# Rotary products from GpSimd to VectorE, and conv taps dealt out anew between the score groups, in a two-layer decoder trunk

## The chip, the cores and the metric

The kernel runs on one core of a Trainium2 chip. The metric is the device time of one execution in microseconds (us). The engines of the core work side by side, each through its own list of instructions in a fixed order: TensorE (PE, with its weight loads PEld), VectorE (DVE), ScalarE (ACT), GpSimd (POOL) and SyncE (SP, which issues DMAs).

## The reference

Two layers over 512 tokens of width 1024, batch 1, in fp32. `q`, `k`, `v`, `u_conv` and `q_mem` are columns of one projection.

```python
for l in range(2):
    h = x + 0.5 * swiglu(rms_norm(x, ffn1_norm[l]), ffn1_w1[l], ffn1_w3[l], ffn1_w2[l])
    n = rms_norm(h, mix_norm[l])
    u_conv, q, k, v, q_mem = split(n @ w_in[l])
    y_conv = silu(layer_norm(causal_depthwise_conv31(glu(u_conv)) + b, g, b2))     # 384 channels
    q = apply_rope(rms_norm(q per head), cos, sin)                                 # 6 heads of 64
    k = apply_rope(rms_norm(k per head), cos, sin)                                 # 2 heads of 64
    y_swa = sliding_window_attention(q, k, v, sinks)                               # blocks of 128
    y_mem = memory_attention(rms_norm(q_mem per head), mk, mv)                     # 4 heads, 256 memory tokens
    h = h + concat(y_conv, y_swa, y_mem) @ w_out[l]
    h = h + 0.5 * swiglu(rms_norm(h, ffn2_norm[l]), ffn2_w1[l], ffn2_w3[l], ffn2_w2[l])
    x = rms_norm(h, final_norm[l])

def apply_rope(x, cos, sin):
    x1, x2 = split(x, 2, axis=-1)
    return concatenate([x1 * cos - x2 * sin, x2 * cos + x1 * sin], axis=-1)
```

## The kernel before

The activations stay on the chip, channels across the 128 partitions and the 512 tokens along them; the weights stream in. Each fp32 product is three passes of TensorE (`mm3`, L176 to L178): an operand is split into a rounded high part and the rest, and hi·hi, hi·lo and lo·hi are summed. A weight tile is split in one of two ways. `split` (L145, L146) rounds on ScalarE and subtracts on VectorE. `split_by_dma` (L150 to L152) rounds on ScalarE, writes the negative on ScalarE as well, and lets a DMA that POOL issues add the raw weights onto it. Activations are split by `split_scaled` (L155 on ScalarE, L156 on VectorE).

A layer is FFN1, the mixer, FFN2. The mixer takes from about 364 to 545 us in layer 0 and 1247 to 1430 us in layer 1. `ORDER` is the list of its steps, and every engine's instructions are issued by a scheduler that follows this list, its queues and the edges that `tc.issue_after` adds:

- `c` projects half a chunk of conv channels; `q` projects a block of 128 tokens' queries and keys and applies the rotary (L701 evacuates, L706 is the product with the sine table on POOL with the halves of each head exchanged, L710 the one with the cosine table, L712 their sum); `Q` transposes them;
- `v` projects a block's values and memory queries (L733, L735 and L548 on ScalarE evacuate them); `V` transposes the memory queries (L581, evacuated by L583);
- `g` begins a group of scores. There are ten groups, of the memory ("r") and of the window ("w"). A group is a few score matmuls (L769, after the mask's L763), maxima on VectorE (L773, L788), and one or two small operations (L774, or L789 and L790) that make the bias of its exponentials (L800);
- `a` is the attention over the groups: exponentials, transposes of the probabilities (L810, evacuated by L812), products with the values (L821), and where a block is complete the division (L830 to L835), its transposes (L844) and the split of the result. `out_weights(d)` fetches and splits the rows of the output weights for the attention's channels, `out_rows` multiplies them;
- `t` adds one chunk's 31 taps of the conv on VectorE (L932 and 30 of L939, over 512 tokens). `EARLY` taps run freely; of the others each is held behind the bias of one group, as many as `LATER` says for it;
- `s` sums the three chunks on POOL (L945 and the line before), takes their mean on TensorE (L950), variance, scale (RL, L221), and Silu.

A step written early can be worked in while TensorE does another, so the order on the engines is not simply that of `ORDER`. The projected weights of the queries, `wqk`, are split by `split_by_dma` for three of their four tiles (hi and lo are called ghi and glo). `Next` prepares the mixer's input while FFN1 ends: for each d the residual h (L475), its split and its Square (L236) for the norm. `factors` gives FFN1 of layer 1 the `after` that scales h with eight VectorE operations (L1053).

Of the kernel before, what the change touches and what calls it, by code (L numbers as in the profile page):

```python
# [64 lines left out]
def trunk(ctx: ExitStack, tc: tile.TileContext, xT, memT, pos, w1a, w3a, w2a, w1b, w3b, w2b,  # L65
# [160 lines left out]
    class Stat:  # L226
# [5 lines left out]
        def square(self, out, src, scale):  # L232
            if self.on:
                self.on.tensor_tensor(out=out, in0=src, in1=src, op=ALU.mult)
            else:
                A.activation(out, src, AF.Square, scale=scale)  # L236
# [104 lines left out]
    def up_pair(l, w13, f, M):  # L341
# [26 lines left out]
        def add(out, a, b):  # L368
            V.tensor_tensor(out=out, in0=a, in1=b, op=ALU.add)  # L369
# [15 lines left out]
        for i in range(2):  # L385
            w = unit(X[i])
            product(xy[i][:, x0], w, 1, 5)
            A.activation(part[i][:, x0], xy[i][:, x0], AF.Copy)
            product(zv[i][:, x1], w, 0, 7)
            add(to[i][:, :, x1], zv[i].rearrange("p (n t) -> p n t", n=2), part[i][:, x0].unsqueeze(1).to_broadcast([P, 2, QT]))  # L390
# [14 lines left out]
    def ffn(l, w13, w2, x, sums, factors, last, at_product, aside=None):  # L405
# [138 lines left out]

    def head_scale(ps, col, n, out=None):

        sq = tm("hsq", "sq", 2)[:, 0 : n * HD]
        A.activation(sq, ps, AF.Square, scale=col)  # L548
# [74 lines left out]
    def mixer(l, x, st, last):  # L623
# [69 lines left out]
        def queries(t):  # L693
            if not t:
                ww["q"] = [weights(wqk[l, i], 1024, G if i else V, spare()) for i in range(4)]
# [8 lines left out]
            for i, (h0, n) in enumerate(((0, NH), (NH, 2))):  # L704
                for half in range(2):
                    G.tensor_tensor(out=q2v[:, h0 : h0 + n, half, :], in0=qv[:, h0 : h0 + n, 1 - half, :],  # L706
                                    in1=sg[:, t, i, half].unsqueeze(1).to_broadcast([P, n, 32]), op=ALU.mult)
# [29 lines left out]

        def value_columns(t):
# [12 lines left out]
        sinks, nsinks = by_half(sink), by_half(nsink[:, l, :])  # L751

        def scored(kind, pairs):
# [33 lines left out]
            for i in range(2):  # L787
                V.tensor_reduce(out=each(nmw, i), in_=pp[i], axis=AX.X, op=ALU.max)  # L788
            V.scalar_tensor_tensor(out=at_(nmw), in0=at_(nmw), scalar=-1.0, in1=rr, op0=ALU.mult, op1=ALU.mult)  # L789
            biased[len(biased)] = V.tensor_tensor(out=at_(nmw), in0=at_(nmw), in1=per(nsinks), op=ALU.min)  # L790
# [32 lines left out]
        def scaled(kind, b, po):  # L823
# [3 lines left out]
            if kind == "w":  # L827
                e = esw[:, b]
                A.activation(e, e, AF.Exp)
# [31 lines left out]
        def attention():  # L861
# [69 lines left out]
        def taps(c):  # L931
            V.tensor_scalar(out=cv[:, c, :], in0=ypad[:, c, 0:S], scalar1=conv_w[:, c, 0:1], scalar2=conv_b[:, c : c + 1],  # L932
                            op0=ALU.mult, op1=ALU.add)
            for j in range(1, TAPS):

                n = c * TAPS + j - EARLY
                group = sum(n >= sum(LATER[:g]) for g in range(1, len(LATER)))
                with tc.issue_after(biased[group].ins) if n >= 0 else nullcontext():
                    V.scalar_tensor_tensor(out=cv[:, c, :], in0=ypad[:, c, j : j + S], scalar=conv_w[:, c, j : j + 1],  # L939
                                           in1=cv[:, c, :], op0=ALU.mult, op1=ALU.add)  # L940


        def swish():
# [18 lines left out]
            with queued():  # L962
                RL = kept(spread(r), "RL")
            for c in range(CC):
                s = ring("cv")
                V.tensor_tensor(out=s, in0=cv[:, c, :], in1=RL, op=ALU.mult)
                A.activation(s, s, AF.Silu, scale=ln_g[:, c : c + 1], bias=ln_b[:, c : c + 1])
                split(y[c][0], y[c][1], s, V)
            for d in range(5, KD):
# [13 lines left out]
        for i, own in enumerate(ours):  # L983
# [3 lines left out]
            A.activation(own[0], raw[:, 0 : 2 * CCH], AF.Copy)  # L987
            A.activation(own[1], raw[:, 0 : 2 * CCH], AF.Copy, scale=-1.0)
# [16 lines left out]
    def stages(st, gain):  # L1005
        def factors(r):
            return gain, kept(spread(r), "R"), lambda: None
# [3 lines left out]
    for l in range(L):  # L1011
# [16 lines left out]
        mixer(l, nxt.x, before, into(gn[:, l, N_FFN2], (st, None)))  # L1028
        sums, factors = stages(st, gn[:, l, N_FFN2])
        st, fin = Stat("st"), gn[:, l, N_FIN]  # L1030
        if l + 1 < L:
# [15 lines left out]
            def factors(r, gg=gg, fin=fin):  # L1047
                R = kept(spread(r[1]), "R")

                def after():  # L1050
                    RF = kept(spread(r[0]), "RL")
                    for d in range(KD):
# [70 lines left out]
```

## Time and profile before

| | |
|---|---|
| median of 3 runs | 1791.62 us (1790.84 to 1792.38) |
| profiled execution | 1790.99 us |
| its span | 1789.2 us |
| granted clock of TensorE | 0.994 |
| busy: PE, PEld, DVE, ACT, POOL | 98%, 88%, 71%, 50%, 11% |

The rows of the profile, in the prediction, read as follows. A row of a timeline has the start, the length, the engine, the line, the operation, what it writes and reads, the tile's shape and the count; in brackets stands how long the engine had been idle and what it waited for. A row of windows has a stretch's bounds, its length, the busy time (and count) of PE, PEld, DVE, ACT and POOL, TensorE's granted clock, the share of the DMA engines and GB/s. A row of a tile or a line has the count, the shortest, median and longest time in ns, and the first and last start. DMA to landing is from a DMA's issue to its last byte.

### The profile page before, as it was taken

The page shows a single profiled execution, that of the slowest core. Times are in us where ns is not written, and L with a number is a line of the kernel's source. Part 1 is how long each engine was busy: PE and PEld are TensorE (multiplying, and loading weights), DVE is VectorE, ACT ScalarE, POOL GpSimd, SP SyncE. Part 2 cuts the span into 40 slices and gives each one's busy share as a digit, 9 for nine tenths or more (in the row PEclk, how much of TensorE's full clock was granted, in tenths as well). Part 3 has the DMA queues.
Part 4 walks back from the last instruction along what each step waited for, and adds up shares of the span by engine and source line. Part 5 has one row for each costly group of instructions (what it writes and reads, how often), then busy time and mean ns, then how long its engine had stood idle before and what let it go on. Part 6 is the DMA issues. An engine that isn't in the chain of part 4 may idle for free.

```text
span 1789.2 us, 28081 instructions
## 1 busy us (share of the span) xinstructions
PE 1757.0 (98%) x11004; PEld 1581.5 (88%) x11004; DVE 1272.3 (71%) x1887; ACT 899.4 (50%) x1367; POOL 194.4 (11%) x217
## 2 busy tenths in 40 slices
PE   8999999999999999999999999999999999999997
PEld 6989999878788989898889898989787889998986
DVE  6969666589947857575678685756797567666755
ACT  6646444464765535353655453535455655453532
POOL 1001000034221000000010000000441210000000
PEclk9999999999999999999999999999999999999998
DMA  9456555183167547464656474643631966574622
GB/s 280 125 163 177 165 139 145 57 217 70 30 176 172 139 136 177 127 173 128 165 136 170 131 190 135 169 114 105 158 70 30 234 127 171 136 183 119 168 74 82
DMA packets 95892, 253.32 MB, mean 142 GB/s; under 512 B 9872, under 2 KB 14224, under 8 KB 95760
## 3 DMA queue, kind: packets, MB, share of 16 engines
q1 hardware_dynamic: 77040, 190.45, 34.9%
q0 software_dynamic: 18720, 61.09, 19.3%
q8 instruction: 86, 1.41, 0.3%
q14 instruction: 46, 0.38, 0.1%
HBM read 249.40 MB, written 2.10 MB: 141 GB/s over the span
## 4 chain that ended last, share of the span: by engine, by line
PE 81%; issue 6%; DVE 6%; DMA 4%; ACT 3%; POOL 0%; SPq 0%; POOLq 0%; DVEq 0%; ACTq 0%
PE mm L177 12%; PE mm L176 11%; PE mm L178 11%; PE po L176 8%; PE po L178 8%; PE po L177 8%; PE pt L176 6%; PE pt L177 6%; PE pt L178 6%; DVE there L939 2%; DMA glo<-in_wqk 1%; DMA raw<-in_wout 1%; DVE wlo L146 1%; PE cf L178 1%; PE cf L176 1%
## 5 line engine op out<-in xcount | busy, mean ns | idle before, releaser
L145 ACT ACTIVATE whi<-raw 128x1024 fp32r<-128x1024 f32 (+3 forms) x344 | 324.5, 945 | 440.5 <-PE mm L177 223.5
L146 DVE TENSOR_TENSOR wlo<-raw,whi 128x1024 fp32r<-128x1024 f32 (+3 forms) x344 | 372.0, 1083 | 133.9 <-ACT whi L145 132.6
L177 PE MATMUL mm<-glo,whi 128*128 128x512 f32 x752 | 293.3, 390 | 0.8 <-DVE glo L146 0.8
L176 PE MATMUL mm<-ghi,whi 128*128 128x512 f32 x752 | 293.3, 392 | 0.0
L178 PE MATMUL mm<-ghi,wlo 128*128 128x512 f32 x734 | 285.7, 389 | 0.9 <-DVE wlo L146 0.9
L177 PE MATMUL po<-ml,whi 128*128 128x256 f32 x864 | 244.5, 283 | 0.0
L178 PE MATMUL po<-mh,wlo 128*128 128x256 f32 x864 | 244.5, 283 | 0.0
L176 PE MATMUL po<-mh,whi 128*128 128x256 f32 x864 | 244.4, 283 | 0.0
L176 PE MATMUL pt<-xhi,whi 128*128 128x256 f32 x864 | 243.3, 283 | 0.6 <-DVE g L369 0.6
L178 PE MATMUL pt<-xhi,wlo 128*128 128x256 f32 x864 | 243.9, 283 | 0.0
L177 PE MATMUL pt<-xlo,whi 128*128 128x256 f32 x864 | 243.9, 283 | 0.0
L475 DVE SCALAR_TENSOR_TENSOR h<-mm,h 128x512 f32<-128x512 f32 x128 | 87.8, 689 | 133.3 <-PE mm L178 133.3
L177 PEld LDWEIGHTS mm<-glo,whi 128*128 128x128 f32 x752 | 141.3, 188 | 29.9 <-DVE glo L146 1.6
L176 PEld LDWEIGHTS mm<-ghi,whi 128*128 128x128 f32 x752 | 141.3, 188 | 29.4 <-DVE h L475 1.2
L176 PEld LDWEIGHTS pt<-xhi,whi 128*128 128x128 f32 x864 | 165.2, 192 | 1.7 <-DVE g L369 0.8
L177 PEld LDWEIGHTS pt<-xlo,whi 128*128 128x128 f32 x864 | 165.7, 192 | 0.8
L176 PEld LDWEIGHTS po<-mh,whi 128*128 128x128 f32 x864 | 165.8, 192 | 0.7
L177 PEld LDWEIGHTS po<-ml,whi 128*128 128x128 f32 x864 | 165.8, 192 | 0.6
L178 PEld LDWEIGHTS po<-mh,wlo 128*128 128x128 f32 x864 | 165.8, 192 | 0.0
L178 PEld LDWEIGHTS pt<-xhi,wlo 128*128 128x128 f32 x864 | 165.6, 192 | 0.0
L178 PEld LDWEIGHTS mm<-ghi,wlo 128*128 128x128 f32 x734 | 137.8, 188 | 30.2 <-DVE wlo L146 1.3
L939 DVE SCALAR_TENSOR_TENSOR there<-ypad,par,there 128x512 f32<-128x512 f32 x180 | 136.7, 770 | 1.6
(312 smaller groups left out, 3312.9 us busy)
## 6 DMA issues: line engine op xcount, KB each, us to landing
raw<-in_w2a SPq DMA_DIRECT2D x48, 384.0 KB, 3.5
raw<-in_w2b SPq DMA_DIRECT2D x48, 384.0 KB, 3.6
raw<-in_w1b SPq DMA_DIRECT2D x26, 512.0 KB, 3.7
raw<-in_w3b SPq DMA_DIRECT2D x26, 512.0 KB, 4.1
raw<-in_w1a SPq DMA_DIRECT2D x25, 512.0 KB, 3.7
raw<-in_w3a SPq DMA_DIRECT2D x25, 512.0 KB, 3.8
wsum<-in_w1a SPq DMA_DIRECT2D x18, 512.0 KB, 4.5
wsum<-in_w3a SPq DMA_DIRECT2D x18, 512.0 KB, 4.4
```

The lines of the kernel that those rows point to most:

```text
L145: A.activation(hi, x, AF.Copy)
L146: on.tensor_tensor(out=lo, in0=x, in1=hi.bitcast(F32), op=ALU.subtract)
L176: T.matmul(ps, a[0], b[0], start=first, stop=False, **more)
L177: T.matmul(ps, a[0], b[1], start=False, stop=False, **more)
L178: tail[0] = T.matmul(ps, a[1], b[0], start=False, stop=last, **more)
L475: added = V.scalar_tensor_tensor(out=h[:, d, :], in0=ps, scalar=0.5, in1=h[:, d, :], op0=ALU.mult, op1=ALU.add)
L939: V.scalar_tensor_tensor(out=cv[:, c, :], in0=ypad[:, c, j : j + S], scalar=conv_w[:, c, j : j + 1], in1=cv[:, c, :], op0=ALU.mult, op1=AL ...
```

## The change

The rotary products with the sine table go from POOL to VectorE: two operations a block (all six query heads, then both key heads) in place of four, in which the exchange of a head's halves is a step of -1. `ORDER`, `EARLY` and `LATER` change. The taps become one list, with those of chunks 1 and 2 alternating near the end, and are laid behind each group's bias with the next group's maxima held behind them; the last 17 stand behind the last group. The output weights 0 to 3 are fetched and split in the steps `v0` and `v2` instead of in the attention. The splits of the query weights 1 to 3 are held behind the norm's last Square, the last pair of the conv's output weights behind the last Silu, and an Exp of the sinks behind the block's last exponential. RL's copy moves to VectorE. The h scaling is done in two halves, after two places of FFN1.

```diff
-ORDER = "c00 c01 q0 c10 q1 c11 Q0 q2 q3 Q1 c20 c21 Q2 v0 v1 V0 Q3 V1 g0 g1 v2 v3 a t0 t1 t2 s"
-EARLY = 49
-LATER = (1, 12, 5, 4, 3, 3, 3, 3, 3, 3)
+ORDER = "c00 c01 q0 c10 q1 c11 Q0 q2 q3 Q1 c20 c21 Q2 v0 v1 V0 Q3 v2 V1 t g0 g1 v3 a s"
+EARLY = 55
+LATER = (0, 8, 4, 3, 2, 1, 1, 1, 1, 17)
...
-                A.activation(out, src, AF.Square, scale=scale)
+                self.done = A.activation(out, src, AF.Square, scale=scale)
...
-                    if f == PLAIN:
-                        with tc.issue_after(M.gated.ins):
-                            after()
+                    if f in (PLAIN, PLAIN + 2):
+                        with tc.issue_after((M.gated if f == PLAIN else M.turned).ins):
+                            after(f > PLAIN)
...
-                ww["q"] = [weights(wqk[l, i], 1024, G if i else V, spare()) for i in range(4)]
+                ww["q"] = []
+                for i in range(4):
+                    with tc.issue_after(operand.stats[0][0].done.ins) if i else nullcontext():
+                        ww["q"].append(weights(wqk[l, i], 1024, G if i else V, spare()))
...
-                for half in range(2):
-                    G.tensor_tensor(out=q2v[:, h0 : h0 + n, half, :], in0=qv[:, h0 : h0 + n, 1 - half, :],
-                                    in1=sg[:, t, i, half].unsqueeze(1).to_broadcast([P, n, 32]), op=ALU.mult)
+                V.tensor_tensor(out=q2v[:, h0 : h0 + n], in0=qv[:, h0 : h0 + n, ::-1, :],
+                                in1=sg[:, t, i].unsqueeze(1).to_broadcast([P, n, 2, 32]), op=ALU.mult)
...
+            for d in {0: (0, 1, 2), 2: (3,)}.get(t, ()):
+                with tc.issue_after((squared[-1] if d > 1 else keyed[2]).ins):
+                    out_weights(d)
...
+        to_do = [(c, j) for c in range(2) for j in range(TAPS)][:EARLY]
+        to_do += [(2, j) for j in range(TAPS - 14)]
+        for j in range(14):
+            to_do += [(1, j) for j in range(j + EARLY - TAPS, TAPS)][:1] if j + EARLY < 2 * TAPS else []
+            to_do.append((2, TAPS - 14 + j))
...
+        def between():
+            return tc.issue_after(tapped[-1].ins) if biased else nullcontext()
+        def taps_behind(small):
+            with tc.issue_after(small.ins):
+                taps(LATER[len(biased)])
+            biased[len(biased)] = small
...
-                for i in range(2):
-                    V.tensor_reduce(out=nmr[:, b, i], in_=pp[i], axis=AX.X, op=ALU.max)
-                biased[len(biased)] = V.scalar_tensor_tensor(out=nmr[:, b], in0=nmr[:, b], scalar=-1.0, in1=by_half(rm[:, b, :]),
-                                                             op0=ALU.mult, op1=ALU.mult)
+                with between():
+                    for i in range(2):
+                        V.tensor_reduce(out=nmr[:, b, i], in_=pp[i], axis=AX.X, op=ALU.max)
+                taps_behind(V.scalar_tensor_tensor(out=nmr[:, b], in0=nmr[:, b], scalar=-1.0, in1=by_half(rm[:, b, :]),
+                                                   op0=ALU.mult, op1=ALU.mult))
...
-                A.activation(e, e, AF.Exp)
+                with tc.issue_after(raised[kind, b, CC - 1].ins):
+                    A.activation(e, e, AF.Exp)
...
-            for d in range(2):
-                with tc.issue_after(keyed[2].ins):
-                    out_weights(d)
...
-                if n in (3, 5):
-                    with tc.issue_after(raised[GROUPS[n - 1][0], *GROUPS[n - 1][-1]].ins):
-                        out_weights(len(out_w))
...
-                RL = kept(spread(r), "RL")
+                RL = kept(spread(r), "RL", V)
...
-            A.activation(own[0], raw[:, 0 : 2 * CCH], AF.Copy)
-            A.activation(own[1], raw[:, 0 : 2 * CCH], AF.Copy, scale=-1.0)
+            with tc.issue_after(silus[0].ins) if i == 3 else nullcontext():
+                A.activation(own[0], raw[:, 0 : 2 * CCH], AF.Copy)
+                A.activation(own[1], raw[:, 0 : 2 * CCH], AF.Copy, scale=-1.0)
...
-                    for d in range(KD):
+                    for d in range(4 * half, 4 * half + 4):
                         V.scalar_tensor_tensor(out=h[:, d, :], in0=h[:, d, :], scalar=fin[:, d : d + 1], in1=RF, op0=ALU.mult, op1=ALU.mult)
```

Three places show how rows move; layer 1 has the same. The numbers in the names tell tiles apart and differ between the two builds.

ScalarE where FFN1 ends and the mixer's input is made, before: ghi and glo are two of the query weights' tiles, xhi and sq are the mixer's input and its Squares.

```order
L150 ACTIVATE ghi_3847<-raw_3849 128x1024
L151 ACTIVATE glo_3848<-raw_3849 128x1024
L155 ACTIVATE xhi_3587<-h_79,gn_80 128x512
L236 ACTIVATE sq_3714<-h_79 128x512
L150 ACTIVATE ghi_3854<-raw_3856 128x1024
L151 ACTIVATE glo_3855<-raw_3856 128x1024
L155 ACTIVATE xhi_3587<-h_79,gn_80 128x512
L236 ACTIVATE sq_3739<-h_79 128x512
L150 ACTIVATE ghi_3861<-raw_3863 128x1024
L151 ACTIVATE glo_3862<-raw_3863 128x1024
```

The same place after:

```order
L155 ACTIVATE xhi_3587<-h_79,gn_80 128x512
L236 ACTIVATE sq_3714<-h_79 128x512
L155 ACTIVATE xhi_3587<-h_79,gn_80 128x512
L236 ACTIVATE sq_3739<-h_79 128x512
L150 ACTIVATE ghi_3847<-raw_3849 128x1024
L151 ACTIVATE glo_3848<-raw_3849 128x1024
L150 ACTIVATE ghi_3854<-raw_3856 128x1024
L151 ACTIVATE glo_3855<-raw_3856 128x1024
L150 ACTIVATE ghi_3861<-raw_3863 128x1024
L151 ACTIVATE glo_3862<-raw_3863 128x1024
```

The six operations of the split weights now stand in one row behind the last Square. On POOL the DMA of the second and third tile stands behind rsq (L193), which it stood ahead of.

TensorE at the start of the attention, before: pt tiles are transposes of memory queries (aux, blocks 0 and 1) and of queries (query), the L769 rows the scores of g0 and g1, po the projection of v2.

```order
L581 MATMUL pt_4281<-cst_96,aux0_3745 128x128 x2
L581 MATMUL pt_4285<-cst_96,query_3750 128x128 x4
L581 MATMUL pt_4292<-cst_96,aux0_3745 128x128 x2
L769 MATMUL mm_4296<-mT_116,there_3743 128x256
L769 MATMUL mm_4297<-mT_116,there_3743 128x256
```

After (the first of v2's 24 matmuls follows the transposes of the queries, the rows here are its last and what follows; pt_4346 are the transposes V1, and po_4431 is v3):

```order
L178 MATMUL po_4305<-ghi_4199,xlo_3588 128x384
L583 MATMUL pt_4346<-cst_96,aux0_3745 128x128 x2
L808 MATMUL mm_4405<-mT_116,there_3743 128x256
L808 MATMUL mm_4406<-mT_116,there_3743 128x256
L808 MATMUL mm_4405<-mT_116,there_3743 128x256
L808 MATMUL mm_4406<-mT_116,there_3743 128x256
L808 MATMUL mm_4414<-mT_116,there_3743 128x256
L808 MATMUL cf_4415<-mT_116,there_3743 128x256
L808 MATMUL mm_4414<-mT_116,there_3743 128x256
L808 MATMUL cf_4415<-mT_116,there_3743 128x256
L176 MATMUL po_4431<-ghi_4180,xhi_3587 128x384
```

ScalarE at this place, after: the evacuation of v2 and a split of output weights (L150, L151) stand ahead of V1's evacuation and the exponentials.

```order
L740 ACTIVATE here_3742<-po_4305,rc_3752 128x2x64
L742 ACTIVATE query_3749<-po_4305,rc_3752 128x256
L550 ACTIVATE hsq_4332<-po_4305,rc_3752 128x256
L150 ACTIVATE whi_4339<-raw_4341 128x640
L151 ACTIVATE wlo_4340<-raw_4341 128x640
L585 ACTIVATE there_3743<-pt_4346 128x2x128
L842 ACT_TABLE_LOAD
```

Before, V1's evacuation directly followed that of the block 3 queries, and v2's came after the exponentials of g0 and g1.

VectorE behind the last bias (the first row in both), before: L939 are taps, rd and aux the division of an attention block, glo its split.

```order
L790 TENSOR_TENSOR nmw_3755<-nmw_3755,nsink_112 128x2
L939 SCALAR_TENSOR_TENSOR there_3743<-ypad_108,par_98,there_3743 128x512
L146 TENSOR_TENSOR glo_4401<-pt_4767,ghi_4400 128x128
L939 SCALAR_TENSOR_TENSOR there_3743<-ypad_108,par_98,there_3743 128x512
L833 RECIPROCAL rd4_4787<-po_4762 128x4
L939 SCALAR_TENSOR_TENSOR there_3743<-ypad_108,par_98,there_3743 128x512
L835 TENSOR_TENSOR aux1_3746<-po_4762,rd4_4787 128x256
L146 TENSOR_TENSOR glo_4399<-pt_4767,ghi_4398 128x2x128
L939 SCALAR_TENSOR_TENSOR there_3743<-ypad_108,par_98,there_3743 128x512 x2
L146 TENSOR_TENSOR glo_4397<-pt_4803,ghi_4396 128x2x128
L146 TENSOR_TENSOR glo_4397<-pt_4808,ghi_4396 128x2x128
L939 SCALAR_TENSOR_TENSOR there_3743<-ypad_108,par_98,there_3743 128x512 x2
```

After, from the third of the groups of taps on (4 and 2 taps, a glo and a division stand ahead of these rows):

```order
L146 TENSOR_TENSOR glo_4468<-pt_4852,ghi_4467 128x2x128
L778 SCALAR_TENSOR_TENSOR there_3743<-ypad_108,par_98,there_3743 128x512
L146 TENSOR_TENSOR glo_4466<-pt_4888,ghi_4465 128x2x128
L778 SCALAR_TENSOR_TENSOR there_3743<-ypad_108,par_98,there_3743 128x512 x2
L146 TENSOR_TENSOR glo_4466<-pt_4893,ghi_4465 128x2x128
L778 SCALAR_TENSOR_TENSOR there_3743<-ypad_108,par_98,there_3743 128x512 x5
L873 TENSOR_TENSOR rd6_4921<-po_4883,esw_3756 128x2x3
L778 SCALAR_TENSOR_TENSOR there_3743<-ypad_108,par_98,there_3743 128x512
L874 RECIPROCAL rd6_4921<-rd6_4921 128x6
L778 SCALAR_TENSOR_TENSOR there_3743<-ypad_108,par_98,there_3743 128x512
L878 TENSOR_TENSOR aux1_3746<-po_4883,rd6_4921 128x384
L778 SCALAR_TENSOR_TENSOR there_3743<-ypad_108,par_98,there_3743 128x512
```

Of 7 taps behind the last bias there are now 17, 16 of them ahead of the last aux; between the first maximum and this place 26 stand where there were 36.

More of the change, by code (lines that the diff above doesn't have):

```diff
@@ L621, in prepare, with mixer @@
         memory(l)
-    def mixer(l, x, st, last):
+    def mixer(l, operand, st, last):
+        x = operand.x
         o = CC * TAPS
@@ L751, in mixer, with taps @@
         sinks, nsinks = by_half(sink), by_half(nsink[:, l, :])
+        to_do = [(c, j) for c in range(2) for j in range(TAPS)][:EARLY]
[3 more added lines that the diff above has]
+            to_do.append((2, TAPS - 14 + j))
+        tapped = []
+        def taps(n=EARLY):
+            for c, j in [to_do.pop(0) for _ in range(n)]:
+                if not j:
+                    t = V.tensor_scalar(out=cv[:, c, :], in0=ypad[:, c, 0:S], scalar1=conv_w[:, c, 0:1], scalar2=conv_b[:, c : c + 1],
+                                        op0=ALU.mult, op1=ALU.add)
+                else:
+                    t = V.scalar_tensor_tensor(out=cv[:, c, :], in0=ypad[:, c, j : j + S], scalar=conv_w[:, c, j : j + 1],
+                                               in1=cv[:, c, :], op0=ALU.mult, op1=ALU.add)
+                tapped.append(t)
+        def between():
[4 more added lines that the diff above has]
+            biased[len(biased)] = small
         def scored(kind, pairs):
@@ L786, in scored @@
                 rr = by_half(rq[:, b, 0:NH])[:, :, c : c + n]
-            for i in range(2):
-                V.tensor_reduce(out=each(nmw, i), in_=pp[i], axis=AX.X, op=ALU.max)
+            with between():
+                for i in range(2):
+                    V.tensor_reduce(out=each(nmw, i), in_=pp[i], axis=AX.X, op=ALU.max)
             V.scalar_tensor_tensor(out=at_(nmw), in0=at_(nmw), scalar=-1.0, in1=rr, op0=ALU.mult, op1=ALU.mult)
-            biased[len(biased)] = V.tensor_tensor(out=at_(nmw), in0=at_(nmw), in1=per(nsinks), op=ALU.min)
+            small = V.tensor_tensor(out=at_(nmw), in0=at_(nmw), in1=per(nsinks), op=ALU.min)
+            taps_behind(small)
             G.tensor_tensor(out=at_(esw), in0=at_(nmw), in1=per(sinks), op=ALU.add)
@@ L928, in out_rows @@
                     mm3(oo[d], at(out_w[d], ALL, blk(n)), y[CC + n], n == CC, False)
[L931 to L940, printed above, removed]
+        silus = []
         def swish():
@@ L1027, in trunk @@
         before, st = st, Stat("st")
-        mixer(l, nxt.x, before, into(gn[:, l, N_FFN2], (st, None)))
+        mixer(l, nxt, before, into(gn[:, l, N_FFN2], (st, None)))
         sums, factors = stages(st, gn[:, l, N_FFN2])
```

20 lines of the change are left out of this document (12 added, 8 removed).

## The prediction

> **What bounds the kernel now.** I read the page first, then the attention and what follows it as windows, then the rows at the places that the change touches, with what each waited for.
>
> ```profile
> PE 1757.0 (98%) x11004; PEld 1581.5 (88%) x11004; DVE 1272.3 (71%) x1887; ACT 899.4 (50%) x1367; POOL 194.4 (11%) x217
> 439.60:486.90 47.30, 44.34 (x328) 37.70 (x325) 45.13 (x99) 34.23 (x77) 9.93 (x11) 0.96 0.15 29
> 486.90:500.50 13.60, 12.23 (x79) 10.56 (x78) 8.06 (x18) 4.58 (x13) 1.92 (x2) 1.00 0.01 1
> 1321.70:1371.20 49.50, 46.55 (x334) 39.74 (x331) 45.68 (x99) 34.34 (x77) 10.48 (x11) 0.93 0.13 27
> ```
>
> TensorE is busy 98% of the span, so only the 32 us in which it isn't, and its slow clock, can be won; the change removes no matmul. VectorE, which is 71% busy over the span, is 95% busy in layer 0's attention (45.13 of 47.30, third number after the stretch's length) from the first maximum to the last bias. Behind it, until TensorE reaches the conv's statistics, VectorE works 8.06 of 13.60 us while TensorE is busy for 12.23. So the taps sit in the stretch where VectorE is dense, and the change moves some of them into a stretch where TensorE is dense and its inputs come from VectorE.
>
> **Query weights.** Three of the four split in three ScalarE and POOL steps: ghi, glo, then a DMA that adds the raw weights onto glo.
>
> ```profile
> 370.42 0.68 DVE L475 SCALAR_TENSOR_TENSOR h<-mm,h 128x512 f32<-128x512 f32 x1
> 370.67 0.61 ACT L236 ACTIVATE sq<-h 128x512 f32<-128x512 f32 x1
> 373.12 0.70 ACT L155 ACTIVATE xhi<-h,gn 128x512 fp32r<-128x512 f32 x1
> 375.20 1.04 ACT L151 ACTIVATE glo<-raw 128x1024 fp32r<-128x1024 f32 x1
> 376.54 0.86 POOL L152 DMA_DIRECT2D glo<-in_wqk  x1 [2.16 <-ACT glo L151]
> 377.10 2.23 POOL L193 TENSOR_TENSOR rsq<-ms,nhalf 128x4 f32<-128x4 f32 x1
> DMA to landing us min/median/max: 8.5/9.4/10.7
> 373.88 0.50 PE L176 MATMUL mm<-xhi,whi 128*128 128x512 f32 x1 [0.46 <-ACT xhi L155]
> 387.28 0.50 PE L177 MATMUL mm<-glo,xhi 128*128 128x512 f32 x1 [0.17 <-DMA glo<-in_wqk]
> 1258.92 0.86 POOL L152 DMA_DIRECT2D glo<-in_wqk  x1 [2.16 <-ACT glo L151]
> 1269.92 0.50 PE L177 MATMUL mm<-glo,xhi 128*128 128x512 f32 x1 [0.41 <-DMA glo<-in_wqk]
> ```
>
> Before, xhi and Square of one column alternate with a split, and TensorE waits at 373.88 for an xhi. After, all the xhi and Squares come first: the last block's input is out at 371.1 (370.42 + 0.68), its xhi and Square take 0.70 and 0.61, so the last Square ends at 372.4 and six splits of 0.96 each (start to start) end at 378.1. The third DMA then goes out at 378.4 instead of 376.54. POOL also has rsq ahead of the second DMA now. This third transfer took 10.7 us (the longest of the three), and TensorE, whose row at 387.28 waited for it by 0.17, waits from then on: 378.4 + 10.7 = 389.1, that is +1.9. What TensorE gains at 373.88 is lost here. In layer 1 the same steps give a DMA at 1260.4 instead of 1258.92, and the wait at 1269.92 moves by as much: +1.4. Bounds: with the shortest landing of the three, 8.5, it would be ready at 386.9 and the term is 0; were three transfers issued closer together to take longer, 12 us, it is +3 each. I take +3.3 for both layers; ends 0 and +6.
>
> **Rotary.** The sixteen POOL products a layer (L706) become eight VectorE ones; the nearest row is the product with the cosine table, of the same shapes.
>
> ```profile
> L706 POOL TENSOR_TENSOR uu<-query,sg x16: 321/741/1170, 392.0 to 421.3; 128x192 f32<-128x192 f32 x8, 128x64 f32<-128x64 f32 x8
> L939 DVE SCALAR_TENSOR_TENSOR there<-ypad,par,there x47: 736/747/1207, 386.8 to 438.9; 128x512 f32<-128x512 f32 x47
> 422.82 0.55 DVE L710 TENSOR_TENSOR query<-query,cg 128x384 f32<-128x384 f32 x1
> 423.49 0.28 DVE L710 TENSOR_TENSOR query<-query,cg 128x128 f32<-128x128 f32 x1
> 437.74 0.42 DVE L550 TENSOR_REDUCE hs<-hsq 128x4 f32<-128x256 f32 x1 [0.99 <-ACT hsq L548]
> ```
>
> Four blocks x (0.47 + 0.20 from start to start) = 2.7 us more on VectorE a layer. Against it, the taps that ran beside L706 were stretched, the longest to 1.21 where the median of 47 is 0.75; for the taps and splits beside the sixteen products I estimate that 0.1 us comes back for each, 1.6 us. The rest, 1.1 us, is hidden: VectorE waits 0.99 us at 437.74 and the first maximum now stands behind 24 more matmuls. Cost 0. No row has a negative step: at twice the price it is +2.7 a layer more, and with the cover gone 1.1; below nothing, the relief alone, -1.6, moves nothing while VectorE is ahead there.
>
> **Attention.** The matmuls of v2 move ahead of the scores of g0 and g1, the four output weights' splits leave the attention (two pairs of ScalarE operations there), and between the first maximum and the last bias stand 26 taps instead of 36.
>
> ```profile
> 438.04 0.44 PE L581 MATMUL pt<-cst,aux 128*128 128x128 f32 x2 [0.81 <-ACT there L583]
> 457.44 0.73 ACT L150 ACTIVATE whi<-raw 128x640 fp32r<-128x640 f32 x1
> 458.71 1.11 PE L821 MATMUL po<-mvn,aux 128*128 128x65 f32 x8 [1.83 <-ACT aux L812]
> 469.58 0.66 PE L810 MATMUL pt<-cst,uu 128*128 128x128 f32 x4 [0.69 <-ACT aux L812]
> 485.02 0.66 PE L810 MATMUL pt<-cst,uu 128*128 128x128 f32 x4 [0.43 <-ACT aux L812]
> 460.72:464.13 3.41, 3.41 (x14) 1.94 (x14) 2.45 (x6) 1.21 (x4) 0.19 (x1) 0.50 0.92 169
> 1341.36:1348.18 6.82, 6.82 (x28) 5.35 (x29) 4.07 (x10) 3.32 (x8) 1.49 (x2) 0.50 0.53 96
> ```
>
> TensorE sets the length of this stretch, since it does the same matmuls and keeps their order but for v2. Its losses in layer 0 are the waits plus 0.16 or so of refilling each: 1.0 + 2.0 + 0.85 + 0.6, and 3.41 us at half the granted clock, which is 1.7; 6.15 in all. In layer 1 the waits are the same, and 6.82 us at half clock make 3.4: 7.85. After, the first wait is covered by v2's matmuls. But the evacuation of V1's transposes stands on ScalarE behind v2's three and the split of the fourth output weight (2 x 0.73), and g1's scores need it: about 1.55 of wait. The exponentials follow later by that, and the first copy that the products need comes about 1.4 late behind them. I keep one slow window of 1.7 and 0.5 of the last wait: 5.15 left. So the last bias comes 1.0 us earlier, in layer 1 1.0 + 1.7 = 2.7 (its second slow window saved). Bounds from the rows: every loss goes, -6.15 and -7.85; or none goes and the new 1.55 comes on top.
>
> **Behind the last bias.** 17 taps instead of 7, laid between what TensorE waits for.
>
> ```profile
> 486.70 0.16 DVE L790 TENSOR_TENSOR nmw<-nmw,nsink 128x2 f32<-128x2 f32 x1
> 486.78 0.75 DVE L939 SCALAR_TENSOR_TENSOR there<-ypad,par,there 128x512 f32<-128x512 f32 x1
> 487.44 0.28 DVE L146 TENSOR_TENSOR glo<-pt,ghi 128x128 fp32r<-128x128 f32 x1
> 491.87 1.53 DVE L939 SCALAR_TENSOR_TENSOR there<-ypad,par,there 128x512 f32<-128x512 f32 x2
> 495.55 0.17 DVE L830 TENSOR_TENSOR rd<-po,esw 128x6 f32<-128x6 f32 x1 [2.16 <-PE po L821]
> 495.98 0.56 DVE L835 TENSOR_TENSOR aux<-po,rd 128x384 f32<-128x384 f32 x1
> 500.52 1.02 PE L950 MATMUL pt<-aux,onesq 128*128 128x512 f32 x2
> ```
>
> Before, the last output block (aux, 495.98) comes 9.1 us behind the bias, after 2.16 idle, and L950 13.7 us behind it. After, 16 taps stand ahead of that aux: 16 x 0.66 (486.78 to 487.44), 4 x 0.12 more where a tap follows one on the same sums (two in 1.53), and 2.1 for the small operations between: 13.1 us. The aux is 4.0 later against the bias; its transposes before stood 0.75 behind its start because TensorE was busy, so 0.2 of that is caught up. TensorE has nothing else in its row, and L950 moves by 3.8. Net of the earlier bias: +2.8 in layer 0, +1.1 in layer 1.
>
> **The rest.**
>
> ```profile
> 519.17 0.58 ACT L221 ACTIVATE RL<-pt 128x512 f32<-128x512 f32 x1
> 527.31 0.50 PE L177 MATMUL mm<-glo,whi 128*128 128x512 f32 x1 [0.28 <-DVE glo L146]
> 967.47 5.38 DVE L1053 SCALAR_TENSOR_TENSOR h<-h,gn,RL 128x512 f32<-128x512 f32 x8
> 976.11 0.50 PE L178 MATMUL mm<-ghi,wlo 128*128 128x512 f32 x1 [0.89 <-DVE wlo L146]
> ```
>
> Eight h scalings of 0.67 stand in one block, and TensorE then loses 0.89 + 0.17 on a split behind them; in two halves that goes, -1.06. RL's copy stood behind the own weights' splits on ScalarE and now runs on VectorE; the waits at 527.31 (0.28 + 0.16) and its twin in layer 1 (0.48 + 0.17) go: -1.1. Both at best; 0 where VectorE, which has more taps just before, is late with the copy. The Exp of esw behind the last raised and the output weights' earlier DMAs cost nothing: ScalarE is busy 34 of 47 us there, and the transfers have 30 us to land.
>
> **Sum.** 3.3 (weights) + 2.8 + 1.1 (attention and tail) - 1.1 (h) - 1.1 (RL) = +5.0 on the profiled execution of 1790.99 us, so 1796.0. The median of the runs shown, 1791.62, lies 0.63 above that execution; I leave that out. About 3.6 us (0.2%) is what a measurement of this kernel can tell from no change.
>
> **Rivals.** *Faster:* with 10 taps and four splits fewer, VectorE and ScalarE feed TensorE in time, and most of its attention losses go with their slow windows. For it: a split (457.44) stands right ahead of the copy that the longest wait (458.71) was for. Against it: V1's evacuation is newly behind such a split. With 6.15 and 7.85 gone, 3.8 paid twice, 2.2 won in the rest and the weights in time, the sum is -8.6: 1782.4. It decides from the point where less than 2.3 us of loss is left in layer 0's attention, since then the bias is earlier by more than the tail's 3.8.
>
> *Same:* the weights land in 8.5 (0), and about half of the attention losses go (-3.1, -3.9), which the tail's 7.6 takes back: 0.6 - 2.2 = 1789.4, and up to 1794 where less of them goes. [...]
>
> *Slower still:* the new waits each start a slow clock, as one of 1.83 us did (3.41 us at 0.50, and 6.82 in layer 1). Candidates are the wait for the third weights, the scores behind V1, and the tail's transposes: two more windows a layer, 4 x 1.7 = 6.8: 1803. [...] *Negative step:* twice the price and no cover, 2 x (1.1 + 2.7) = +7.6, also about 1803; no row speaks for it.
>
> **Chances.** My forecast 0.32, faster 0.25, same 0.27, slower still 0.13, negative step 0.03. Faster by over 0.2% is 0.25; the same 0.28, with a little of the forecast's lower end; slower 0.47. The range runs from the faster rival to the slow windows, 1782 to 1803; the forecast's own is 1793 to 1800.
>
> **What would show it.** Waits of TensorE for glo from in_wqk over 1.5 us near 389 and 1271; the last bias about 1 us earlier against the first scores' transposes; taps dense to about 13 us behind it, TensorE waiting there for the last aux; no L706 on POOL, eight products of 0.55 and 0.28 on VectorE, and taps all at 0.75 there; no wait near 976. I am wrong if the stall near 458 is gone with its slow clock and nothing takes its place, or if the weights land in time.

## The result

The changed kernel takes 1808.84 us (median of 4 runs, 1806.09 to 1810.06), the kernel before beside it 1791.23 (4 runs). The ratio is 1.0096, 95% interval 1.0078 to 1.0113: slower by 1%, where 1796.0 was forecast and 1803 was the range's upper end. The profiled execution after took 1806.09 us, span 1804.0, granted clock 0.993.

First what TensorE waited for (us in total, times, longest):

```profile
PE mm L177 <- DMA glo<-in_wqk: 7.5, 5, 2.2
PE mm L176 <- ACT xhi L155: 6.1, 1, 6.1
PE pt L887 <- DVE aux L878: 4.8, 2, 3.1
PE mm L808 <- ACT there L585: 2.9, 2, 1.4
PE pt L887 <- DVE glo L146: 2.5, 2, 1.3
PE po L863 <- ACT aux L854: 2.3, 2, 1.6
```

The query weights, 0.6 us before, are now the longest, and the tail's transposes (L887) wait for VectorE. (The second row is the program's first matmul, which waited 6.3 us before too.) TensorE executes the same 11,004 matmuls, nearly all in the same order, so the two traces can be laid on each other: how much later the same matmul starts after than before, at places where that changes (layer 0, layer 1):

| place | shift at its start | at its end |
|---|---|---|
| xhi, ahead of the query weights | 0.4, 8.9 | -0.6, 7.6 |
| query weights | -0.6, 7.6 | 6.1, 12.9 |
| attention, up to behind the last score's transposes | 6.1, 12.9 | 4.5, 9.4 |
| tail, up to the mean's matmul | 4.5, 9.4 | 9.2, 15.7 |
| conv output, RL and Silu | 9.2, 15.7 | 10.1, 16.3 |
| h scaling in FFN1 of layer 1 | 10.1 | 8.9 |
| the rest of layer 1 | 16.3 | 14.7 |

The weights bring 6.7 and 5.2, the tail 4.7 and 6.3, the attention -1.6 and -3.5; the waits for xhi ahead of the weights, 1.0 and 1.2, are won, as forecast. Of the clock, windows answer (the last three numbers of a row are the granted clock, the DMA share and GB/s):

```profile
388.40:391.90 3.50, 2.41 (x7) 1.34 (x6) 2.44 (x4) 1.68 (x3) 0.86 (x1) 0.50 1.05 269
391.90:395.30 3.40, 3.40 (x8) 2.73 (x9) 0.03 (x1) 3.40 (x5) 1.19 (x2) 0.51 0.99 238
1283.00:1286.40 3.40, 3.40 (x10) 2.62 (x10) 1.93 (x4) 2.02 (x3) 0.86 (x1) 0.54 1.05 249
449.00:491.50 42.50, 39.45 (x301) 32.90 (x302) 37.75 (x88) 31.87 (x73) 7.06 (x8) 1.00 0.08 16
491.50:509.80 18.30, 14.67 (x83) 12.45 (x83) 15.54 (x28) 4.75 (x13) 3.19 (x3) 0.91 0.01 1
1395.20:1398.70 3.50, 3.50 (x11) 2.82 (x12) 1.16 (x3) 0.66 (x2) 1.28 (x1) 0.52 0.00 0
```

The attention (449.00 to 491.50) runs at full clock. That it is shorter than the 47.30 of before is mostly v2's 24 matmuls, which now stand ahead of it. The tail is 18.30 long where it was 13.60. The half clock now stands behind the query weights and in both tails.

The rows at the weights (timeline, and the tile's landings):

```profile
372.14 0.62 ACT L236 ACTIVATE sq<-h 128x512 f32<-128x512 f32 x1
376.06 1.03 POOL L193 TENSOR_TENSOR rsq<-ms,nhalf 128x4 f32<-128x4 f32 x1 [0.24 <-DVE ms L208]
378.74 0.87 POOL L152 DMA_DIRECT2D glo<-in_wqk  x1 [0.78 <-ACT glo L151]
DMA to landing us min/median/max: 9.2/11.0/13.1
388.11 0.57 PE L177 MATMUL mm<-glo,xhi 128*128 128x512 f32 x1 [2.21 <-DMA glo<-in_wqk]
391.89 0.80 PE L177 MATMUL mm<-glo,xhi 128*128 128x512 f32 x1 [1.09 <-DMA glo<-in_wqk]
```

The last Square ends at 372.8 and the third DMA goes out at 378.74, as worked out (372.4, 378.4), but it takes 13.1 us instead of 10.7, the second is waited for as well, and TensorE, which is at half clock from 388 to 395, is slow in between. Windows from the first of the three DMAs' issue to the last one's landing, before and after:

```profile
370.45:387.24 16.79, 15.92 (x76) 12.39 (x74) 9.05 (x16) 10.41 (x13) 4.51 (x4) 1.00 0.94 253
374.96:391.85 16.89, 13.22 (x58) 9.90 (x57) 9.29 (x14) 9.54 (x11) 4.50 (x5) 0.90 0.97 240
```

The group of transfers takes as long as before, though the DMAs go out closer together, and the DMA engines are busy 0.94 and 0.97 of the time, with raw loads beside the three. So the last landing moved by 4.6 us, as the first issue did (4.5), and not by the last issue's 2.2. In layer 1 the group takes 17.0 us before and 15.6 after, at 0.92 and 0.98, and its last landing moved by 11.3 us, between the first issue's 12.7 and the last one's 10.4.

The tail on VectorE, POOL and TensorE:

```profile
498.80 1.27 POOL L972 TENSOR_TENSOR aux<-there 128x512 f32<-128x512 f32 x1 [6.58 <-DVE there L778]
498.97 4.79 DVE L778 SCALAR_TENSOR_TENSOR there<-ypad,par,there 128x512 f32<-128x512 f32 x5
505.25 0.55 DVE L878 TENSOR_TENSOR aux<-po,rd 128x384 f32<-128x384 f32 x1
505.95 0.30 PE L887 MATMUL pt<-cst,aux 128*128 128x128 f32 x1 [1.67 <-DVE aux L878]
1395.13 0.50 PE L887 MATMUL pt<-cst,aux 128*128 128x128 f32 x2 [3.13 <-DVE aux L878]
```

The last bias ends at 491.49, the last aux starts 13.8 behind it (13.1 was forecast). The five taps from 498.97 take 4.79 where five at the 0.79 of before, from start to start, make 3.9: the first of them is stretched to 1.64 beside POOL's sum of chunks 0 and 1 (L972), and the same in layer 1. The sum waits for chunk 1's last tap. Before (L945) it stood at 454 in the attention. Since taps of chunk 1 now alternate with chunk 2's, it comes into the tail.

### The profile page after: what moved, and what is told of

It is laid out like the page before. It is cut to its first block, busy times and chain, and to the rows that moved or that the text cites. A ratio compares the mean times of both kernels' runs of the same rounds, so it can differ in the third digit from the quotient of the medians.

```text
span 1804.0 us, 28056 instructions
## 1 busy us (share of the span) xinstructions
PE 1761.2 (98%) x11004; PEld 1583.3 (88%) x11004; DVE 1276.5 (71%) x1905; ACT 898.4 (50%) x1365; POOL 175.4 (10%) x185
## 4 chain that ended last, share of the span: by engine, by line
PE 80%; DVE 7%; issue 6%; DMA 4%; ACT 2%; SPq 0%; POOL 0%; POOLq 0%; DVEq 0%; ACTq 0%
PE mm L177 11%; PE mm L176 11%; PE mm L178 11%; PE po L178 8%; PE po L176 8%; PE po L177 8%; PE pt L177 5%; PE pt L178 5%; PE pt L176 5%; DVE there L778 2%; DMA glo<-in_wqk 1%; DVE wlo L146 1%; DMA raw<-in_w3a 1%; PE cf L177 1%; PE cf L176 1%
```

## The experiments

Times below are medians, with the ratio to the kernel before on the same chip; the profiled execution of a kernel lies up to 4.1 us off its median, to either side.

**Query weights.** `e1_no_hold` takes the hold out of the changed kernel, `e4_hold_only` puts it alone into the kernel before, `e7_hold_no_dma` keeps it but splits on VectorE, so that no DMA stands behind the splits.

```diff
-                    with tc.issue_after(operand.stats[0][0].done.ins) if i else nullcontext():
+                    with nullcontext():                                                  # e1
-                        ww["q"].append(weights(wqk[l, i], 1024, G if i else V, spare()))
+                        ww["q"].append(weights(wqk[l, i], 1024, V, spare()))             # e7
```

> The changed kernel, but the splits of the query weights are no longer held behind the norm's last Square. Theory (held splits send the three adding DMAs out late, TensorE waits for the last two and then runs 3.4 us or more at half clock): TensorE's shift against before grows by 6.6 us in layer 0 and 3.8 in layer 1 at this place, so the time falls by about 10.4, from 1806 to 1809 down to 1796 to 1798; no wait of TensorE on glo<-in_wqk over 0.5 us, and a clock of 1.00 between 386 and 396. Rival (the transfers are late because other loads moved, not because of the hold): the third still takes over 11 us to land, and the time stays above 1803.

> The kernel before with one part of the change alone: query weights 1 to 3 split behind the norm's last Square. Theory (this part alone costs what the trace of the changed kernel shows at the place): 10.4 us, 1800 to 1803, with two waits a layer of 1 to 2.5 us on glo<-in_wqk and a half clock behind them. Rival (it costs only the shift of the last landing, as forecast): 1794 to 1796. Rival (only together with the other moved DMAs): 1790 to 1793.

> The changed kernel, with the hold, but query weights 1 to 3 are split by VectorE (rounded on ScalarE, subtracted on VectorE) in place of the adding DMAs. Theory (the loss comes from the landing, 9 to 13 us behind the held splits): no wait on glo<-in_wqk, clock 1.00 from 386 to 396, and 9 to 11 us less than the changed kernel, 1797 to 1799; three subtractions of 1.2 us fit into VectorE's waits there. Rival (the splits themselves come too late on ScalarE): a wait of 1 us or more on the glo of VectorE takes the place, and the time stays above 1803.

Measured: e1 1796.20 us (1.0035, 1.0022 to 1.0048), e4 1797.60 (1.0047, 1.0031 to 1.0063), e7 1794.19 (1.0013, 1.0005 to 1.0022). Windows of e1, then of e7, at the place, and TensorE's wait in e4:

```profile
386.00:396.00 10.00, 10.00 (x45) 8.00 (x44) 9.48 (x16) 6.82 (x8) 2.65 (x3) 1.00 0.79 194
```

```profile
383.00:396.00 13.00, 13.00 (x59) 10.77 (x58) 11.79 (x21) 7.47 (x9) 3.39 (x4) 1.00 0.72 172
```

```profile
PE mm L177 <- DMA glo<-in_wqk: 8.1, 6, 2.2
```

Taking the hold out wins 12.6 us, and keeping it without the DMAs 14.6: the splits on ScalarE are early enough, it is the landing of what follows them. In e1 and e7 TensorE is busy without a gap at clock 1.00. Not all of e1's 12.6 is the weights': its tails are 17.5 and 16.7 us long, those of the changed kernel 18.3 and 19.9. Alone the hold costs 6.7 us, less than the theory's 10.4: its profiled execution, at 1801.70, has both the waits (8.1 us) and the half clock (0.50 from 391.40 to 394.80), but three of its six runs lie at 1795 to 1796.3. What differs in those runs, no profile shows.

**The tail.** `e2_tail7` sets `LATER = (0, 8, 5, 5, 4, 3, 2, 2, 2, 7)` in the changed kernel; `e12_tail_only` sets `LATER = (1, 8, 4, 3, 2, 2, 2, 2, 2, 17)` in the kernel before.

> The changed kernel with LATER = (0, 8, 5, 5, 4, 3, 2, 2, 2, 7): 7 taps behind the last bias as before, the other ten spread over the groups. Theory (the 17 taps make the last aux late): the tail's +4.7 and +6.2 us fall to 1 at most, no wait of the last transposes on aux over 0.3. If the attention's gain (1.5 and 3.5 us) came from its lighter VectorE, it is given back and the time is about 1800 to 1803; if it came from the output weights' splits leaving ScalarE there, it stays and the time is 1795 to 1798. Rival (the tail is slow for another reason, such as TensorE's clock): above 1804.

> The kernel before with one part of the change alone: LATER = (1, 8, 4, 3, 2, 2, 2, 2, 2, 17), 17 taps behind the last bias; here twelve of them stand ahead of the last aux and all are of one chunk. Theory (what is taken out of the attention shortens it by less than the tail grows, since TensorE sets the attention's length and waits for VectorE in the tail): 1 to 2.5 us less a layer up to the last bias, 2.5 to 4.5 more from there to the mean's matmul, 1792 to 1796. Rival (without the hold and the rotary VectorE has room, and the lighter attention pays): 1786 to 1790.

Measured: e2 1801.32 us (1.0066, 1.0049 to 1.0083), e12 1796.27 (1.0023, 1.0013 to 1.0034). Windows of e12, first maximum to last bias and from there to the mean's matmul, and its waits:

```profile
440.30:484.60 44.30, 42.38 (x325) 36.38 (x322) 38.10 (x88) 33.85 (x77) 9.24 (x11) 1.00 0.15 31
484.60:502.20 17.60, 13.13 (x83) 10.64 (x82) 16.13 (x31) 5.40 (x13) 2.34 (x2) 1.00 0.02 3
```

```profile
PE pt L950 <- POOL aux L946: 5.3, 2, 2.6
```

From the last bias to the mean's matmul it is 13.7 us with 7 taps (13.6 in e2) and 17.5 in e12, 18.3 and 19.9 in the changed kernel. From the first maximum to the last bias 47.3 and 49.0 become 44.3 and 44.3 in e12, so 3.0 and 4.7 are won and 3.8 lost twice. But 1.7 and 3.4 of what is won are the half-clock stretches (3.41 and 6.82 us at 0.50) that the profile before has there and e12's (1.00) has not. Without them 1.3 a layer is won, and the tail costs 2.5 more than it brings, 5.0 over both layers, beside 4.3 by the medians. In e12 the wait is for POOL's final sum, since the taps end the chain there; in the changed kernel it was for the last aux. In e2 the attention is longer again (44.8 us in both layers, 42.5 and 42.2 in the changed kernel) and TensorE's waits for the copies of the probabilities grow from 3.9 to 6.4 us in all; so of the tail's 11.0 us e2 wins 7.5. The theory's first branch holds: a good part of the attention's gain was VectorE's.

**The rotary.** `e5_rotary_only` has the VectorE products alone in the kernel before; `e10_after_pool` puts the POOL products back into the changed kernel.

> The kernel before with one part of the change alone: the rotary products on VectorE, two a block with the step of -1. Theory (covered): VectorE's products take 0.55 and 0.28, the taps beside them all 0.75, and the time is within 1.5 us of before. Rival (VectorE is longer by what isn't given back, 1.1 us a layer, with no cover): 1793 to 1794. Rival (the relief of the taps counts more): 1788 to 1789.

> The changed kernel with the rotary products back on POOL, four operations a block, and nothing else undone. Theory (VectorE has no slack in the mixer: what the rotary takes ahead of the first maximum displaces taps into the attention, as the 44 against 47 taps of e5_rotary_only and the 50 against 53 of e8_v1_first and e9_v1_first_pool show): about 3 more taps ahead of the first maximum and 3 to 6 us less than the changed kernel, 1802 to 1806. Rival (behind the tail's 17 taps VectorE has room in the attention, so that the displaced taps cost nothing here): within 1.5 us of the changed kernel.

Measured: e5 1794.22 us (1.0024, 1.0015 to 1.0034), e10 1804.90 (1.0075, 1.0060 to 1.0091), so 3.3 and 3.9 us, and my cost of nothing is refuted by e5. The 3.9 alone would not do it: the intervals of e10 and of the changed kernel (1.0078 to 1.0113) overlap, and e10's runs fall into two groups, at 1799 and at 1804 to 1806. But its attentions take 39.8 us in both layers instead of 42.5 and 42.2, with 52 taps ahead of the first maximum instead of 48. By line, VectorE's rows in the 55 us ahead of the first maximum of layer 0, before and then in e5 (busy, mean ns, idle before):

```profile
L939 DVE SCALAR_TENSOR_TENSOR there<-ypad,par,there 128x512 f32<-128x512 f32 x47 | 35.5, 774 | 0.4
```

```profile
L938 DVE SCALAR_TENSOR_TENSOR there<-ypad,par,there 128x512 f32<-128x512 f32 x44 | 31.7, 745 | 0.3
L705 DVE TENSOR_TENSOR uu<-query,sg 128x384 f32<-128x384 f32 (+1 forms) x8 | 3.0, 419 | 1.0 <-ACT query L701 1.0
L685 DVE TENSOR_TENSOR aux<-mm,R 128x512 f32<-128x512 f32 x3 | 2.1, 687 | 0.5 <-PE mm L178 0.4
```

The step of -1 costs nothing (0.42 on average, as the product with the cosine table), and the taps are relieved, 0.774 to 0.745. But three taps less fit ahead of the first maximum, 44 for 47, since VectorE now also waits for ScalarE's evacuation of the queries (1.0), which POOL used to do. These three taps stand in the attention, which takes 48.7 us from the first maximum to the last bias instead of 47.3. In layer 1 it takes 48.5 instead of 49.0, with one half-clock stretch where the profile before has two (granted clock of the whole executions 0.995 and 0.994); without these stretches' loss it is 1.4 us longer in layer 0 and 1.2 in layer 1.

**The rest, and a faster version.** `e6_undo_three` undoes hold, tail and the own weights' hold. `e8_v1_first` also puts V1 ahead of v2 in `ORDER`, `e9_v1_first_pool` further puts the rotary back on POOL, and `e11_pool_tail9` moves two more taps behind the last bias. `e3_own_early` undoes in the changed kernel only the hold of the last own weights' split.

```diff
-ORDER = "... Q3 v2 V1 t g0 g1 v3 a s"
+ORDER = "... Q3 V1 v2 t g0 g1 v3 a s"
-            with tc.issue_after(silus[0].ins) if i == 3 else nullcontext():
+            with nullcontext():
```

> The changed kernel with three parts undone: no hold of the query weights, 7 taps behind the last bias (the other ten spread as in e2_tail7), and the last own weights' split no longer held behind the last Silu. Theory (hold and tail hold nearly all of the loss, and the attention gives back what it won when the taps return): within 2 us of before, 1789 to 1793, with TensorE still waiting 1.4 us a layer for V1's evacuation. Rival (a third cost is in the rest of the change, the rotary on VectorE first): 1794 to 1797.

> As e6_undo_three, with V1 ahead of v2 in ORDER, so that its transposes are evacuated ahead of v2's columns and of the split of the fourth output weight. Theory (the wait of g1's scores is that evacuation's place on ScalarE): no wait of L808 on L585, and 2 to 3 us less than e6_undo_three over both layers. Rival (the exponentials' chain behind it sets the pace anyway): the wait goes to the first copies of the probabilities, the same time within 1 us.

> As e8_v1_first, with the rotary products back on POOL (four operations a block). Theory (the measured 3.3 us of the rotary alone come from VectorE being dense with taps until the first maximum): here too 2 to 3 us less than e8_v1_first. Rival (with v2's matmuls ahead of the scores the eight operations are covered, and the 3.3 us were the slow windows of single runs): within 1 us of e8_v1_first, or 1 us more.

> As e9_v1_first_pool, with LATER = (0, 8, 5, 5, 3, 3, 2, 2, 1, 9): 9 taps behind the last bias in place of 7. Theory (behind the last bias VectorE is idle for about 2 us before the last division, so two taps fit there, and the attention is shorter by what they took): 0.5 to 2 us less a layer, 1783 to 1786. Rival (TensorE waits of the tail follow at once): 1787 to 1789.

> The changed kernel with the last own weights' split no longer held behind the last Silu. Theory (held, it stands on ScalarE ahead of the last ghi, and TensorE waits 0.75 us for the glo that follows): the wait at about 537 falls below 0.35, as before, and its twin in layer 1 too; 1 to 1.5 us in all, too little for one time to tell. Rival (RL's copy on VectorE is what is late): the waits stay.

Measured: e6 1791.69 us (0.9999, 0.9989 to 1.0010), e8 1793.32 (1.0014, 1.0004 to 1.0024), e9 1786.70 (0.9973, 0.9964 to 0.9983), e11 1793.32 (1.0014, 1.0004 to 1.0024); e3 1804.03, one run. So undoing the three parts takes back the whole loss, and what the rest of the change costs and wins comes out at nothing. V1's place is worth nothing by itself: the scores no longer wait for L585 in e8 (2.9 us in e6), but V1's transposes do (1.6), and the copies of the probabilities are waited for 6.4 us instead of 5.3. e9 is faster than both kernels by the interval, and against e8 the rotary costs 6.6 us: 53 taps ahead of the first maximum on POOL, 50 on VectorE. The clock is not the reason: their profiles are 6 us apart, at granted clocks of 0.996 (e8) and 0.997 (e9), and have one half-clock stretch each ahead of the program's last waits. Windows of e9, attention and tail of layer 0 and layer 1:

```profile
444.70:486.80 42.10, 39.29 (x300) 32.76 (x296) 40.23 (x93) 31.44 (x73) 8.62 (x9) 1.00 0.07 17
486.80:500.40 13.60, 12.68 (x83) 10.86 (x82) 7.91 (x18) 4.77 (x13) 1.92 (x2) 1.00 0.00 1
1325.30:1367.40 42.10, 39.29 (x300) 32.76 (x297) 40.23 (x93) 31.44 (x73) 8.64 (x9) 1.00 0.08 17
1367.40:1381.00 13.60, 12.68 (x83) 10.86 (x82) 7.91 (x18) 4.77 (x13) 1.93 (x2) 1.00 0.01 2
```

No slow window is left in its attentions, and the tail is as short as before. The two taps of e11 were expected to be free and are not, and it is slower than its rival had it, too: its tail in layer 0 has a stretch at half clock (492.40 to 495.90, 0.53) behind waits of the transposes. In layer 1, without one, the tail takes 14.4 us instead of 13.6 and the attention 41.6 instead of 42.0, so the taps cost 0.4 there. Where the rest of e11's loss stands, one profile of each can't say.

In e3 TensorE's waits for glo are 0.2 and 0.4 us in the two layers instead of 0.75 and 0.74, but this does not show the theory. Rows of the changed kernel:

```profile
529.58 1.06 ACT L145 ACTIVATE whi<-raw 128x1024 fp32r<-128x1024 f32 x1 [5.42 <-DMA raw<-in_w1b]
534.85 0.61 ACT L145 ACTIVATE ghi<-aux 128x512 fp32r<-128x512 f32 x1
535.36 1.22 DVE L146 TENSOR_TENSOR wlo<-raw,whi 128x1024 fp32r<-128x1024 f32 x1
536.20 0.83 ACT L1016 ACTIVATE whi<-raw 128x768 fp32r<-128x768 f32 x1
536.50 0.68 DVE L146 TENSOR_TENSOR glo<-aux,ghi 128x512 fp32r<-128x512 f32 x1
536.93 0.83 ACT L1017 ACTIVATE whi<-raw 128x768 fp32r<-128x768 f32 x1
537.23 0.51 PE L177 MATMUL mm<-glo,whi 128*128 128x512 f32 x1 [0.75 <-DVE glo L146]
```

The glo that ends the wait (536.50) belongs to the ghi at 534.85, ahead of the held split (536.20), and stands on VectorE behind the split of another weight (535.36). Nor do the waits go with the hold: e1 and e7 keep it and have 0.31 and 0.39, and none and 0.20; e11 has not got it and has 0.74 and 0.76. They go with a load. The split at 529.58 waits for raw<-in_w1b, and the Silus stand behind it on ScalarE. In layer 0 it starts 19.8 us behind the mean's matmul in the changed kernel and in e11, 18.9 in e1, 18.8 in e3 and 18.6 in e7. What moves that landing, no run separates.

## Why the prediction was wrong

The sign was right. What failed is the step from issue to landing for the query weights, the cover of the rotary, and the waits at RL; the tail was right in mechanism and too small.

- **Query weights, +1.9 and +1.4: failed, the largest miss.** TensorE is 5.7 and 4.0 later behind them than before (6.7 and 5.2 lost, 1.0 and 1.2 won at xhi); that it is the landing, e1 and e7 show. The ScalarE and POOL times were right to 0.4 us. The step that fell is 378.4 + 10.7 = 389.1: I let the last transfer take what it had taken and moved it by its own delay, 1.9. The DMA engines were nearly full already before (0.94), and in layer 0 the last landing moved as the first issue did, by 4.6. TensorE waits for each of the transfers, 3.7 us a layer in all, and then runs 6.8 us at half clock in layer 0 and 3.4 in layer 1, which I had left to a rival.
- **Rotary, 0: failed.** The step that fell is "the rest is hidden". VectorE's one wait ahead of the first maximum was no cover: the taps fill what is free there, and in e5 the products (3.0 us) and their waits (1.0) displace three taps, 44 for 47, into the attention. The bound without cover, 1.1 a layer, was too low as well; it left out the wait for the queries (1.0 in e5). 3.3 alone, 6.6 in e8 against e9.
- **Attention, -1.0 and -2.7: the size came out, the parts did not, so this was luck.** It is -1.6 and -3.5. I kept one half-clock stretch of 1.7 in each layer; the changed kernel's attentions have none, which alone is 1.7 and 3.4 against the profile before. The rest, which was to win 1.0 a layer, won nothing; with the products on POOL, e10's attentions are 2.7 and 2.5 us shorter. The wait of 1.55 for V1's evacuation was right (1.43). Nor are the stretches a fixed price of this code: e6 has the same attention in both layers, at a clock of 0.93 (46.9 us) in layer 0 and of 1.00 (44.9 us) in layer 1.
- **Tail, +3.8: right in mechanism, low in size** (4.7 and 6.3). The last aux came 0.7 later than worked out, for the tap stretched to 1.64 beside POOL's sum. Both tails have a half clock of 3.4 us; layer 0's begins at 497.6, ahead of the last wait (1.67), layer 1's behind it (3.13), where it adds its 1.7 in full.
- **h scaling, -1.1: right** (10.1 to 8.9). **RL, -1.1: failed** (0.9 and 0.6 lost). RL's copy does come earlier, 14.7 us behind the mean's matmul instead of 18.7. But the step from it to the waits fell: the Silus stand behind a split that waits for raw<-in_w1b, and that starts 19.8 us behind the matmul where it was 19.1. The cause of this delay stays open.

Of the rivals, two gave 1803. The negative step is refuted (0.42, as without). That of more slow windows, at 0.13, came nearest, but not by its own sum: over both mixers 17.1 us at half clock stand where 10.2 stood, a loss of 3.4 more and not 6.8. That the weights land in 8.5, as the rival of the same time had it, is refuted: these DMAs took 9.2 to 13.1 us in layer 0 and 8.0 to 11.8 in layer 1.

## What to carry to other kernels

Where one engine has elastic filler work (here the taps), an idle gap of it need not be cover: VectorE waited 0.99 us at 437.74 before, and e5's products still displaced three taps and cost 3.3 us. So cost an added operation as the filler that it displaces, at the place where that filler ends up. With the DMA engines 0.94 busy before and 0.97 after, the last landing of the group moved by 4.6 us in layer 0, as the group's first issue did (4.5), and not by its own issue's 2.2; in layer 1, at 0.92 and 0.98, by 11.3, between 12.7 and 10.4. So ask when a group of transfers begins, and for every consumer that waits, not the last one. Work behind the last input of a stage is not free because the engine has idle time there: VectorE had 2.16 us of it before, and with e11's two taps layer 1's tail takes 14.4 us instead of 13.6.

## What was not expected of the hardware

The half clock does not follow the length of a wait alone. Behind 2.21 and 3.13 us it came, as quoted; waits of 1.43 and 1.65 in the changed kernel's attentions left it at 1.00. But in e1 it came behind 0.25 us of wait among the one-column matmuls of a norm (e1's row, the 3.4 us behind it, and then the same place before):

```profile
903.77 1.05 PE L202 MATMUL cf<-onesq,RL 128*128 128x1 f32 x8 [0.25 <-DVE ms L208]
```

```profile
904.70:908.10 3.40, 3.40 (x10) 2.71 (x10) 0.66 (x4) 1.29 (x2) 2.96 (x4) 0.51 0.93 216
```

```profile
902.60:906.00 3.40, 3.40 (x16) 2.77 (x16) 0.44 (x3) 0.80 (x1) 2.49 (x3) 1.00 0.91 205
```

The wait there is 0.25 us in the profiles before (ahead of 901.18) and after (ahead of 911.27) as well, and both stay at 1.00, after from 909.00 to 918.00; e1's edit doesn't touch this place. Nor had TensorE been idle for long: of the 3.40 us from 900.40 to 903.80 in e1 it was busy for 3.15. So whether a stretch follows differs from profile to profile, with the same code and the same wait at the place; what decides it, no run shows.

The trace's clock records give the stretches ahead of the program's last waits: before, 3.413 us from 460.72 and 6.827 from 1341.36; after, 6.827 us from 388.39 and 3.413 each from 497.62, 1282.68 and 1395.32. In these two profiles the starts lie whole multiples of 3.413 us apart, 258 before, 32, 230 and 33 after.

Such stretches are a candidate for the scatter of single runs, 1787 to 1797 us for the kernel before; no run tests it. A difference of one or two stretches between two single profiles, 1.7 us each (3.41 us at 0.50), need not be an effect of the change.
